# Layer-1 norms on one activation table, context statistics moved between the latent steps, and a gate weight piece moved ahead of the key rotation

## The chip, the cores and the metric

The kernel runs on one core of a Trainium2 chip. The metric is the device time of one execution in microseconds (us); lower is better. The engines are TensorE (PE, matmuls), VectorE (DVE), ScalarE (ACT), GpSimd (POOL) and SyncE (SP, which issues the DMAs). Each engine runs its own instructions in order, and they wait for one another by semaphores.

## What is computed

Two layers over 256 latent tokens and 256 context tokens with 1024 features. Layer 0 mixes with windowed attention and a gated recurrence, layer 1 with retention; each ends with a SwiGLU network. Ahead of every matrix product stands an RMS norm with a shift and a scale:

```python
def rms_norm(x, g=None):
    y = xf * lax.rsqrt(jnp.mean(xf * xf, axis=-1, keepdims=True) + EPS)
...
h_lat = modulate(rms_norm(x, norm_g[layer, 0]), m_lat[0], m_lat[1])
h_ctx = modulate(rms_norm(ctx, norm_g[layer, 0]), m_ctx[0], m_ctx[1])
...
q_l = apply_rope(to_heads(p['q'], RET_HEADS), cos, sin)
k_l = apply_rope(to_heads(p['k'], RET_HEADS), cos, sin) * k_scale
...
y_lat = gated_head_norm(o_fw + flip(o_bw), p['g']).astype(dt) @ w_out
```

## The kernel before

Features lie on the partitions and tokens along the free axis. Weights come in a fixed order as pieces of eight 128x128 blocks: SP loads a piece (`raw`, three buffers), ACT copies it to a rounded upper half (`whi`, L270) and DVE subtracts that from the raw piece for the lower half (`wlo`, L271), four buffers of each. A product is three matmuls: upper by upper (L343), upper weight by lower activation (L344), lower weight by upper activation (L345); where both halves of the activation lie side by side, two (L340 and L341).

Most code is written in program order and a list scheduler places instructions on the engines. On DVE and ACT the code of the first retention head (`ret_kq`, `ret_gate`, `ret_scores` for head 0) keeps its written order, which includes the norms that it drains first.

At the start of layer 1 there are two norms. The latent one (stream 0, lane `b`) keeps its matmuls ahead of its statistics: `pre` gives x times the gain, `first_group` multiplies four columns of weights by that (96 matmuls of 258 columns on `mm` banks, for two key and two query columns), and `fix` (L473, L474) applies the reciprocal root to the result. The same norm also builds the normed latents `hh`/`hl`, which the rest of the layer reads: for each of eight 128-feature slices `scaled` (L493, DVE), `shifted` (L499 on ACT for the upper half, L500 on DVE for the lower). The context norm (stream 1, lane `c`) has no `pre`; its eight steps of L493, L499, L500 must be done before the 48 context matmuls, which use the same weights and go to `ax` banks. `Norm.stats` is the statistics: a matmul with ones (L487), the logarithm (`ln`, L296 in the manual part) and the exponential (L490). `ln` loads the activation table for the logarithm (L294), and the table for the exponential is loaded ahead of L490.

After that come on DVE the four `fix` pairs, on ACT the bias of each (L1122), the rotation of the keys (`rope`, six DVE operations L1095 to L1097), two weight pieces by two calls of `ensure`, the rotation of the queries, and the splits; on TensorE the gate columns of head 0 (`ret_gate`) with the transposes of the normed tokens (`tok_lane`, L1110 and L1111) among them, and then the scores.

The norm ahead of the layer-1 FFN is the same class with `l = 1, j = 1`: `first_group` without context, latents only. There DVE's `join` additions (L357) and the FFN's products follow. `look` is how many pieces `ensure` prepares ahead.

Of the kernel before, what the change touches and what calls it, by code (L numbers as in the profile page):

```python
# [17 lines left out]
D = 1024  # L18
# [50 lines left out]
def hybrid_kernel(ctx, tc, xT, wst, mw0, mwT, small, cbc, cst, imask, dmat, out, order):  # L69
# [15 lines left out]
    def nm(s):  # L85
        uid[0] += 1
        return f"{s}_{uid[0]}"
# [7 lines left out]
    def mmb():  # L95
        return pm.tile([P, NT], F32, tag="mm", name=nm("mm"))
# [46 lines left out]
    epst = cp.tile([P, 1], F32, tag="eps", name="eps")  # L143
# [108 lines left out]
    pieces = {}  # L252
# [10 lines left out]
    def ensure(p):  # L263
        for q in range(len(pieces), min(p + look[0], N_PIECE - 1) + 1):
            r = q
            load_raw(r)
            src = raws.pop(r)
            hi = wp.tile([P, PIECE, P], F32R, tag="whi", name=nm("whi"))
            lo = wp.tile([P, PIECE, P], F32R, tag="wlo", name=nm("wlo"))
            A.activation(hi[:], src[:], AF.Copy)  # L270
            V.tensor_tensor(lo[:], src[:], hi[:].bitcast(F32), ALU.subtract)  # L271
            pieces[q] = (hi, lo)
# [26 lines left out]
    lanes = {}  # L299
# [23 lines left out]
    def drain(lane):  # L323
        q = lanes.get(lane, [])
        while q:
            for _ in q.pop(0):
                pass
# [19 lines left out]
    def cut(a, s):  # L347
        return (a[0][:, s], a[1][:, s])
# [53 lines left out]
    def first_group(src, cols, nl, hs, n_ctx):  # L402

        if nl.l > nl.j:
            look[0] = 0
            ensure(len(pieces))
            drain('b')
            ensure(len(pieces))
            drain('c')
        ps = [mmb() for _ in cols]  # L410
        ws = {}
        tail = 3 if nl.l and nl.j else 0
        todo = [(i, j) for i in range(KD - tail) for j in range(len(cols))]
        todo += [(i, j) for j in range(len(cols)) for i in range(KD - tail, KD)]
        for i, j in todo:
            ws[i, j] = take(src, i, cols[j])
            mm3(ps[j][:, 0:LW], ws[i, j], nl.p[i], i == 0, i == KD - 1)
        drain('b')
        lat = [nl.fix(p) for p in ps]
        drain('c')  # L420
        ctx = [(axb if j < FA else mmb)()[:, 0:L] for j in range(n_ctx)]
        if nl.l:
            todo = [(i, j) for i in K8 for j in range(n_ctx)]
        else:
            todo = [(i, j) for j in range(n_ctx) for i in K8]
        for i, j in todo:
            mm3(ctx[j], ws[i, j], cut(hs[i], CTX), i == 0, i == KD - 1)
        return lat, ctx
# [24 lines left out]
    class Norm:  # L453
# [31 lines left out]
        def stats(self):  # L485
            ps = axb()[:, 0:L]
            T.matmul(ps, ones, self.acc, start=True, stop=True)  # L487
            self.r = u()[:, 0:L]
            ln(self.r, ps, after=self.last, bias=epst[:], scale=1.0 / D)
            A.activation(self.r, self.r, AF.Exp, scale=-0.5)  # L490

        def scaled(self, k, t):
# [8 lines left out]

        def finish(self):
            self.stats()
            ahead = []
            for k in range(KD):
                if self.p:
                    yield
                t = u()[:, 0:L]
                self.scaled(k, t)
                ahead.append((k, t))  # L510
                if len(ahead) > (self.l > self.j):
                    self.shifted(*ahead.pop(0))
            for a in ahead:
                self.shifted(*a)
# [432 lines left out]
    for hd in range(4):  # L947
        c = E_H + 3 * hd
# [168 lines left out]
    def ret_kq(hd):  # L1117
        c = 12 * hd
        if hd == 0:
            lat, kc = first_group('oin', [c + O_K, c + O_K + 1, c + O_Q, c + O_Q + 1], n1[0], HS, 2)  # L1120
            for t, b in lat:
                A.activation(t, t, AF.Identity, bias=b)  # L1122
            (k0, _), (k1, _), (q0, _), (q1, _) = lat
            push('t', tok_lane())
        else:
            pk = group('oin', [c + O_K, c + O_K + 1], K8, HS, kouter=False)
            k0, k1 = pk[0][:, LAT], pk[1][:, LAT]
            kc = [pk[0][:, CTX], pk[1][:, CTX]]
        kf = [u(), u()]
        kk = []  # L1130
        rope([kf[0][:, LAT], kf[1][:, LAT]], k0, k1)
        qf = u((P, 2, L))
        if hd == 0:
            ensure(len(pieces))
            ensure(len(pieces))
            look[0] = LOOK
            rope([qf[:, 0, :], qf[:, 1, :]], q0, q1)
        for i in range(2):
            A.activation(kf[i][:, CTX], kc[i], AF.Copy)
            hi, lo = u(dt=F32R), u(dt=F32R)  # L1140
            split(kf[i][:], hi[:], lo[:])
            kk.append((hi[:], lo[:]))
        if hd:
            pq = group('oin', [c + O_Q, c + O_Q + 1], K8, HS, sls=(LAT,), kouter=False)
            q0, q1 = pq[0][:, LAT], pq[1][:, LAT]
            rope([qf[:, 0, :], qf[:, 1, :]], q0, q1)
        qhi, qlo = u((P, 2, L), F32R), u((P, 2, L), F32R)
        split(qf[:], qhi[:], qlo[:])
        return kk, (qhi, qlo)
# [240 lines left out]
```

## Time and profile before

| | |
|---|---|
| median of 3 runs | 1142.93 us (1140.12 to 1144.97) |
| profiled execution, whole | 1142.81 us |
| profiled execution, span of the trace | 1141.0 us, so 1.81 us lie around it |
| TensorE busy | 1112.6 us, 98% of the span |
| VectorE, ScalarE busy | 798.0 us (70%), 567.8 us (50%) |
| mean granted clock of TensorE | 0.994 |

The busy share of TensorE is not its peak, but the times at which it stands still are plain in the trace: what it waits for ends the kernel later. Times in the rows below are microseconds from the start of the span. PEclk is the clock that TensorE was granted, 1.00 for 2.4 GHz and 0.50 for 1.2 GHz.

### The profile page before, as it was taken

The numbers are of one execution on the slowest core, as the hardware profiler recorded it, in microseconds if no ns is written. First come the engines' busy times: TensorE is split into PE (matmuls) and PEld (weight loads), VectorE is DVE, ScalarE is ACT, GpSimd is POOL, SyncE is SP. The second block draws the span as 40 slices with busy tenths as digits, with TensorE's granted clock in tenths as the row PEclk, the third lists the DMA queues.
The fourth block names the chain that finished last, engine by engine and source line by source line (L and its number), as shares of the span: only waits on it lengthen the run. The fifth ranks groups of instructions, "written<-read, shape, count | busy, mean of one in ns | idle before, by whom it ended". The sixth has DMA issues, their size and how long they took to land.

```text
span 1141.0 us, 17472 instructions
## 1 busy us (share of the span) xinstructions
PE 1112.6 (98%) x6762; PEld 959.2 (84%) x6762; DVE 798.0 (70%) x1479; ACT 567.8 (50%) x996; POOL 20.9 (2%) x46
## 2 busy tenths in 40 slices
PE   3999999999999999999999998999999999999998
PEld 1777878888998888888888898999989889888887
DVE  3877698999798557347884568474747498767665
ACT  5676676673753222122232466454545566654651
POOL 0012000000000000000000000000000000000000
PEclk9899999999999999999999998999999999999999
DMA  9987212325327456247994323343434364665663
GB/s 327 353 236 185 93 57 75 101 86 186 109 95 250 138 161 207 75 129 221 316 311 128 95 91 111 111 130 121 125 125 131 110 185 156 212 186 185 187 186 108
DMA packets 56115, 182.37 MB, mean 160 GB/s; under 512 B 6368, under 2 KB 9824, under 8 KB 55904
## 3 DMA queue, kind: packets, MB, share of 16 engines
q1 hardware_dynamic: 53648, 176.45, 48.5%
q0 software_dynamic: 2240, 4.72, 1.7%
q8 instruction: 53, 0.87, 0.3%
q14 instruction: 30, 0.25, 0.1%
q10 hardware_dynamic: 144, 0.08, 0.0%
HBM read 177.56 MB, written 1.05 MB: 157 GB/s over the span
## 4 chain that ended last, share of the span: by engine, by line
PE 86%; DVE 8%; ACT 3%; issue 1%; DMA 1%; DVEq 0%; ACTq 0%; SPq 0%
PE mm L345 16%; PE mm L343 16%; PE mm L344 16%; PE mm L340 13%; PE mm L341 7%; PE ax L344 2%; PE ax L345 2%; PE ax L343 2%; PE ax L340 1%; DVE wlo L271 1%; PE ax L175 1%; DVE u L493 1%; PE ax L695 1%; DMA raw<-in_wst_dram 1%; PE ax L714 1%
## 5 line engine op out<-in xcount | busy, mean ns | idle before, releaser
L270 ACT ACTIVATE whi<-raw 128x1024 fp32r<-128x1024 f32 x230 | 243.1, 1058 | 358.5 <-PE mm L344 173.7
L271 DVE TENSOR_TENSOR wlo<-raw,whi 128x1024 fp32r<-128x1024 f32 x230 | 280.7, 1223 | 132.9 <-ACT whi L270 130.3
L343 PE MATMUL mm<-hh,whi 128*128 128x512 f32 (+1 forms) x752 | 273.3, 364 | 3.6 <-ACT whi L270 3.6
L344 PE MATMUL mm<-hl,whi 128*128 128x512 f32 (+1 forms) x752 | 272.7, 363 | 0.0
L345 PE MATMUL mm<-hh,wlo 128*128 128x512 f32 (+1 forms) x752 | 272.0, 362 | 0.5 <-DVE wlo L271 0.3
L343 PEld LDWEIGHTS mm<-hh,whi 128*128 128x128 f32 x752 | 144.0, 192 | 24.5 <-ACT whi L270 4.1
L345 PEld LDWEIGHTS mm<-hh,wlo 128*128 128x128 f32 x752 | 143.8, 191 | 22.0 <-DVE wlo L271 1.1
L344 PEld LDWEIGHTS mm<-hl,whi 128*128 128x128 f32 x752 | 144.0, 192 | 20.0 <-issue 0.2
L340 PE MATMUL mm<-u,whi 128*128 128x512 f32 x368 | 131.5, 398 | 0.5 <-DVE u L451 0.5
L344 PE MATMUL mm<-u,whi 128*128 128x512 f32 (+2 forms) x336 | 114.5, 341 | 0.0
L345 PE MATMUL mm<-u,wlo 128*128 128x512 f32 (+2 forms) x336 | 114.4, 341 | 0.0
L343 PE MATMUL mm<-u,whi 128*128 128x512 f32 (+2 forms) x336 | 114.1, 341 | 0.0
L340 PE MATMUL mm<-hh,whi 128*128 128x512 f32 x320 | 112.5, 396 | 0.9 <-DVE u L357 0.9
L341 PE MATMUL mm<-u,wlo 128*128 128x256 f32 x368 | 103.0, 280 | 0.0
L233 DVE CUSTOM_DVE_ANT_0 mr<-mr,cb 128x1024 f32<-128x1024 f32 x72 | 87.2, 1223 | 15.1 <-DMA mr<-in_mwT_dram 14.4
L341 PE MATMUL mm<-hh,wlo 128*128 128x256 f32 x320 | 89.4, 281 | 0.0
L340 PEld LDWEIGHTS mm<-u,whi 128*128 128x128 f32 x368 | 69.1, 188 | 16.3 <-DVE u L451 0.8
L340 PEld LDWEIGHTS mm<-hh,whi 128*128 128x128 f32 x320 | 60.0, 188 | 15.4 <-DVE u L357 1.2
L343 PEld LDWEIGHTS mm<-u,whi 128*128 128x128 f32 x336 | 63.5, 189 | 7.3
L341 PEld LDWEIGHTS mm<-u,wlo 128*128 128x128 f32 x368 | 69.5, 189 | 0.1
L344 PEld LDWEIGHTS mm<-u,whi 128*128 128x128 f32 x336 | 63.6, 189 | 7.0
L345 PEld LDWEIGHTS mm<-u,wlo 128*128 128x128 f32 x336 | 63.5, 189 | 7.1
(238 smaller groups left out, 1664.0 us busy)
## 6 DMA issues: line engine op xcount, KB each, us to landing
raw<-in_wst_dram SPq DMA_DIRECT2D x230, 512.0 KB, 3.7
mr<-in_mwT_dram SPq DMA_DIRECT2D x80, 512.0 KB, 4.6
u<-in_mw_dram SPq DMA_DIRECT2D x16, 256.0 KB, 5.2
u<-u POOLq DMA_DIRECT2D x20, 128.0 KB, 6.0
u<-in_dmat_dram POOLq DMA_DIRECT2D x8, 256.0 KB, 3.1
raw<-in_mw_dram SPq DMA_DIRECT2D x6, 256.0 KB, 5.2
mr<-in_mw_dram SPq DMA_DIRECT2D x6, 256.0 KB, 5.2
x<-in_xT_dram SPq DMA_DIRECT2D x8, 128.0 KB, 3.6
```

What stands on the lines that cost most here:

```text
L175: T.matmul(ps[32 * g:32 * g + 32, :], cT[:, k, :], mws[nt * 8 + k], start=(k < 4), stop=(k >= 4), skip_group_check=True)
L233: V.tensor_tensor_reduce(o, mr[:], cb[:, s, :], 1.0, 0.0, ALU.mult, ALU.add, mvec(l, s, ch, k))
L270: A.activation(hi[:], src[:], AF.Copy)
L271: V.tensor_tensor(lo[:], src[:], hi[:].bitcast(F32), ALU.subtract)
L340: T.matmul(o, w[0], a[2], start=first, stop=False, skip_group_check=True)
L341: anchor[0] = T.matmul(o[:, 0:L], w[1], a[0], start=False, stop=last, skip_group_check=True)
L343: T.matmul(o, w[0], a[0], start=first, stop=False, skip_group_check=shared)
L344: T.matmul(o, w[0], a[1], start=False, stop=False, skip_group_check=shared)
L345: anchor[0] = T.matmul(o, w[1], a[0], start=False, stop=last, skip_group_check=shared)
L493: V.scalar_tensor_tensor(t, xs(k, self.s), gsv[:, self.l, self.j, self.s, k:k + 1], self.r, ALU.mult, ALU.mult)
L695: T.transpose(tp[:, i, :], p[:, i * P:(i + 1) * P], ident)
L714: T.matmul(o[64 * j:64 * j + 64, col:col + P], vtok[:, kk, 64 * j:64 * j + 64], pts[3 * j + w][:, blk, :], start=(n == 0), stop=last, skip ...
```

## The change

The statistics of every layer-1 norm take one table that holds both functions. The context norm yields after its statistics, and `first_group` of the layer-1 mixer advances lane `b` three times and then lane `c` once before it drains `b`. One of the two `ensure` calls of `ret_kq` moves to the place right after `first_group`.

```diff
--- before.py
+++ after.py
@@ -404,6 +404,9 @@
         if nl.l > nl.j:
             look[0] = 0
             ensure(len(pieces))
+            for _ in range(3):
+                next(lanes['b'][0])
+            next(lanes['c'][0])
             drain('b')
             ensure(len(pieces))
             drain('c')
@@ -486,7 +489,7 @@
             ps = axb()[:, 0:L]
             T.matmul(ps, ones, self.acc, start=True, stop=True)
             self.r = u()[:, 0:L]
-            ln(self.r, ps, after=self.last, bias=epst[:], scale=1.0 / D)
+            ln(self.r, ps, after=self.last, exp=self.l > 0, bias=epst[:], scale=1.0 / D)
             A.activation(self.r, self.r, AF.Exp, scale=-0.5)
 
         def scaled(self, k, t):
@@ -501,6 +504,8 @@
 
         def finish(self):
             self.stats()
+            if self.l > self.j and not self.p:
+                yield
             ahead = []
             for k in range(KD):
                 if self.p:
@@ -1118,6 +1123,7 @@
         c = 12 * hd
         if hd == 0:
             lat, kc = first_group('oin', [c + O_K, c + O_K + 1, c + O_Q, c + O_Q + 1], n1[0], HS, 2)
+            ensure(len(pieces))
             for t, b in lat:
                 A.activation(t, t, AF.Identity, bias=b)
             (k0, _), (k1, _), (q0, _), (q1, _) = lat
@@ -1131,7 +1137,6 @@
         rope([kf[0][:, LAT], kf[1][:, LAT]], k0, k1)
         qf = u((P, 2, L))
         if hd == 0:
-            ensure(len(pieces))
             ensure(len(pieces))
             look[0] = LOOK
             rope([qf[:, 0, :], qf[:, 1, :]], q0, q1)
```

ScalarE at the start of layer 1, from the fifth latent step on (`hh_725` is the upper half of the fifth normed slice; `whi_1188` is the fourth weight piece of the group; `ax_1190` the context's sum of squares; `hh_717<-u_1192` the first context step). Before:

```order
L499 ACTIVATE hh_725_3430<-u_1183_6245,modv_175 128x256
L499 ACTIVATE hh_727_3432<-u_1184_6249,modv_175 128x256
L499 ACTIVATE hh_729_3434<-u_1185_6253,modv_175 128x256
L499 ACTIVATE hh_731_3436<-u_1186_6257,modv_175 128x256
L270 ACTIVATE whi_1188_6265<-raw_1187_6263 128x1024
L294 ACT_TABLE_LOAD
L296 ACTIVATE u_1191_6271<-ax_1190_6269,eps_173 128x256
L490 ACT_TABLE_LOAD
L490 ACTIVATE u_1191_6271<-u_1191_6271 128x256
L499 ACTIVATE hh_717_3422<-u_1192_6275,modv_175 128x256
L499 ACTIVATE hh_719_3424<-u_1193_6277,modv_175 128x256
```

And now (the fourth piece is `whi_1190` here, the context's sum `ax_1185`):

```order
L502 ACTIVATE hh_725_3430<-u_1183_6245,modv_175 128x256
L294 ACT_TABLE_LOAD
L296 ACTIVATE u_1186_6255<-ax_1185_6253,eps_173 128x256
L493 ACTIVATE u_1186_6255<-u_1186_6255 128x256
L502 ACTIVATE hh_727_3432<-u_1184_6249,modv_175 128x256
L502 ACTIVATE hh_729_3434<-u_1187_6259,modv_175 128x256
L502 ACTIVATE hh_731_3436<-u_1188_6263,modv_175 128x256
L270 ACTIVATE whi_1190_6271<-raw_1189_6269 128x1024
L502 ACTIVATE hh_717_3422<-u_1192_6275,modv_175 128x256
```

The context's table load, logarithm and exponential moved ahead of the sixth latent step, the load ahead of the exponential is gone, and the fourth weight piece comes after them.

VectorE behind the context steps, from the last `fix` (L474, `u_1210`) on; L1095 to L1097 (L1100 to L1102 in the changed file) are rotations. Before, both gate pieces (`wlo_1221`, `wlo_1224`) stand behind the keys' rotation:

```order
L474 TENSOR_TENSOR u_1210_6419<-mm_1203_6310,u_1173_6149 128x256
L1095 TENSOR_TENSOR u_1216_6479<-u_1204_6407,con_84 128x256
L1096 TENSOR_TENSOR u_1216_6479<-u_1206_6411,con_84 128x256
L1097 TENSOR_TENSOR u_1214_6477<-u_1216_6479 128x256
L1095 TENSOR_TENSOR u_1217_6483<-u_1206_6411,con_84 128x256
L1096 TENSOR_TENSOR u_1217_6483<-u_1204_6407,con_84 128x256
L1097 TENSOR_TENSOR u_1215_6478<-u_1217_6483 128x256
L271 TENSOR_TENSOR wlo_1221_6491<-raw_1219_6488,whi_1220_6490 128x1024
L271 TENSOR_TENSOR wlo_1224_6497<-raw_1222_6494,whi_1223_6496 128x1024
L1095 TENSOR_TENSOR u_1225_6500<-u_1208_6415,con_84 128x256
L1096 TENSOR_TENSOR u_1225_6500<-u_1210_6419,con_84 128x256
```

And now:

```order
L477 TENSOR_TENSOR u_1210_6419<-mm_1203_6310,u_1173_6149 128x256
L271 TENSOR_TENSOR wlo_1216_6476<-raw_1214_6473,whi_1215_6475 128x1024
L1100 TENSOR_TENSOR u_1219_6485<-u_1204_6407,con_84 128x256
L1101 TENSOR_TENSOR u_1219_6485<-u_1206_6411,con_84 128x256
L1102 TENSOR_TENSOR u_1217_6483<-u_1219_6485 128x256
L1100 TENSOR_TENSOR u_1220_6489<-u_1206_6411,con_84 128x256
L1101 TENSOR_TENSOR u_1220_6489<-u_1204_6407,con_84 128x256
L1102 TENSOR_TENSOR u_1218_6484<-u_1220_6489 128x256
L271 TENSOR_TENSOR wlo_1224_6497<-raw_1222_6494,whi_1223_6496 128x1024
L1100 TENSOR_TENSOR u_1225_6500<-u_1208_6415,con_84 128x256
```

The first gate piece (`wlo_1216`) moved ahead of the six operations of the keys' rotation; the second kept its place. TensorE at the same place, the first gate matmuls (`mm_1233` the first gate column, `mm_1234` the second). Before:

```order
L343 MATMUL mm_1233_6522<-hh_717_3422,whi_1220_6490 128x256
L344 MATMUL mm_1233_6522<-hl_718_3423,whi_1220_6490 128x256
L343 MATMUL mm_1234_6523<-hh_717_3422,whi_1223_6496 128x256
L344 MATMUL mm_1234_6523<-hl_718_3423,whi_1223_6496 128x256
L345 MATMUL mm_1233_6522<-hh_717_3422,wlo_1221_6491 128x256
L1110 MATMUL ax_1238_6533<-idr_6231,hh_717_3422 128x128
```

And now:

```order
L343 MATMUL mm_1233_6522<-hh_717_3422,whi_1215_6475 128x256
L344 MATMUL mm_1233_6522<-hl_718_3423,whi_1215_6475 128x256
L345 MATMUL mm_1233_6522<-hh_717_3422,wlo_1216_6476 128x256
L1115 MATMUL ax_1238_6533<-idr_6231,hh_717_3422 128x128
L1116 MATMUL ax_1238_6533<-idr_6231,hl_718_3423 128x128
```

The two matmuls of the second gate column that stood between now come later with the rest of that column.

VectorE in the layer-1 FFN's first group, from the `fix` of the last columns on (`wlo_1781` and `wlo_1784` are the third and fourth pieces of the next group of columns). Before:

```order
L473 COPY s_1767_9518<-mm_1740_9358 128x1
L474 TENSOR_TENSOR u_1766_9517<-mm_1740_9358,u_1745_9367 128x256
L493 SCALAR_TENSOR_TENSOR u_1768_9521<-x5_91,gsv_176,u_1745_9367 128x256
L493 SCALAR_TENSOR_TENSOR u_1769_9525<-x6_92,gsv_176,u_1745_9367 128x256
L493 SCALAR_TENSOR_TENSOR u_1770_9529<-x7_93,gsv_176,u_1745_9367 128x256
L500 SCALAR_TENSOR_TENSOR hh_1654_8905<-u_1768_9521,modv_175,hh_1654_8905 128x256
L500 SCALAR_TENSOR_TENSOR hh_1655_8906<-u_1769_9525,modv_175,hh_1655_8906 128x256
L500 SCALAR_TENSOR_TENSOR hh_1656_8907<-u_1770_9529,modv_175,hh_1656_8907 128x256
L271 TENSOR_TENSOR wlo_1781_9552<-raw_1779_9549,whi_1780_9551 128x1024
L271 TENSOR_TENSOR wlo_1784_9574<-raw_1782_9571,whi_1783_9573 128x1024
```

And now:

```order
L476 COPY s_1765_9514<-mm_1739_9357 128x1
L477 TENSOR_TENSOR u_1764_9513<-mm_1739_9357,u_1745_9367 128x256
L271 TENSOR_TENSOR wlo_1781_9552<-raw_1779_9549,whi_1780_9551 128x1024
L476 COPY s_1767_9518<-mm_1740_9358 128x1
L477 TENSOR_TENSOR u_1766_9517<-mm_1740_9358,u_1745_9367 128x256
L496 SCALAR_TENSOR_TENSOR u_1768_9521<-x5_91,gsv_176,u_1745_9367 128x256
L496 SCALAR_TENSOR_TENSOR u_1769_9525<-x6_92,gsv_176,u_1745_9367 128x256
L496 SCALAR_TENSOR_TENSOR u_1770_9529<-x7_93,gsv_176,u_1745_9367 128x256
L503 SCALAR_TENSOR_TENSOR hh_1654_8905<-u_1768_9521,modv_175,hh_1654_8905 128x256
L503 SCALAR_TENSOR_TENSOR hh_1655_8906<-u_1769_9525,modv_175,hh_1655_8906 128x256
L503 SCALAR_TENSOR_TENSOR hh_1656_8907<-u_1770_9529,modv_175,hh_1656_8907 128x256
L271 TENSOR_TENSOR wlo_1784_9574<-raw_1782_9571,whi_1783_9573 128x1024
```

The third piece moved from behind the last three slices' steps (three L493, three L500) to a place ahead of them.

## Rows read from the trace of the kernel before

**Rows 1.** Waits of TensorE by releaser: us in total, times, longest us.

```profile
PE ax L487 <- DVE u L483: 17.7, 2, 11.2
PE mm L343 <- ACT whi L270: 3.6, 3, 2.3
PE mm L340 <- DVE u L357: 0.9, 1, 0.9
```

**Rows 2.** Windows: us, busy of PE, PEld, DVE, ACT, POOL, PEclk, DMA share, GB/s.

```profile
691.00:691.50 0.50, 0.44 (x2) 0.24 (x2) 0.47 (x2) 0.50 (x1) 0.00 (x0) 0.93 0.00 0
691.50:698.00 6.50, 5.96 (x26) 5.67 (x27) 6.43 (x13) 3.92 (x8) 0.00 (x0) 0.50 0.51 161
698.00:698.50 0.50, 0.50 (x5) 0.50 (x5) 0.50 (x1) 0.27 (x1) 0.00 (x0) 0.75 0.00 0
909.00:911.00 2.00, 1.54 (x8) 1.36 (x9) 2.00 (x8) 1.98 (x5) 0.00 (x0) 1.00 0.69 219
972.00:974.00 2.00, 1.14 (x7) 0.77 (x6) 2.00 (x5) 1.84 (x4) 0.00 (x0) 1.00 0.39 70
```

**Rows 3.** Timeline of TensorE, context matmuls to scores: start us, us, instruction [idle before].

```profile
682.25 0.40 PE L343 MATMUL ax<-hh,whi 128*128 128x256 f32 x2
...
688.35 0.28 PE L345 MATMUL ax<-hh,wlo 128*128 128x256 f32 x1
690.94 0.39 PE L343 MATMUL mm<-hh,whi 128*128 128x256 f32 x1 [2.31 <-ACT whi L270]
...
692.83 0.58 PE L345 MATMUL mm<-hh,wlo 128*128 128x256 f32 x1
...
699.91 0.28 PE L343 MATMUL mm<-hh,whi 128*128 128x256 f32 x1
...
701.35 0.22 PE L1110 MATMUL ax<-idr,hh 128*128 128x128 f32 x1
...
702.20 0.33 PE L343 MATMUL mm<-hh,whi 128*128 128x256 f32 x1
...
703.33 0.28 PE L343 MATMUL ax<-u,u 128*128 128x256 f32 x1
```

**Rows 4.** Timeline of ScalarE, layer-1 norms.

```profile
666.07 1.28 ACT L490 ACT_TABLE_LOAD   x1
...
673.44 0.51 ACT L499 ACTIVATE hh<-u,modv 128x256 fp32r<-128x256 f32 x1 [0.62 <-DVE u L493]
...
676.23 1.04 ACT L270 ACTIVATE whi<-raw 128x1024 fp32r<-128x1024 f32 x1
...
678.59 0.47 ACT L296 ACTIVATE u<-ax,eps 128x256 f32<-128x256 f32 x1
...
680.38 0.42 ACT L490 ACTIVATE u<-u 128x256 f32<-128x256 f32 x1
```

**Rows 5.** Timeline of VectorE, context steps to key rotation.

```profile
680.83 0.88 DVE L493 SCALAR_TENSOR_TENSOR u<-u,gsv,u 128x256 f32<-128x256 f32 x2 [2.29 <-ACT u L490]
...
687.72 0.15 DVE L473 COPY s<-mm 128x1 f32<-128x1 f32 x1
...
689.30 0.41 DVE L1095 TENSOR_TENSOR u<-u,con 128x256 f32<-128x256 f32 x1
...
691.56 2.35 DVE L271 TENSOR_TENSOR wlo<-raw,whi 128x1024 fp32r<-128x1024 f32 x2
...
696.09 1.89 DVE L451 TENSOR_TENSOR u<-u,u 128x512 fp32r<-128x512 f32 x3
```

**Rows 6.** Timelines of VectorE, ScalarE, TensorE, start of layer-1 FFN.

```profile
964.54 2.36 DVE L271 TENSOR_TENSOR wlo<-raw,whi 128x1024 fp32r<-128x1024 f32 x2
...
970.36 1.06 ACT L270 ACTIVATE whi<-raw 128x1024 fp32r<-128x1024 f32 x1 [2.22 <-DMA raw<-in_wst_dram]
...
972.93 0.75 DVE L357 TENSOR_TENSOR u<-u,mm 128x256 f32<-128x256 f32 x2
...
973.40 0.50 PE L340 MATMUL mm<-hh,whi 128*128 128x512 f32 x1 [0.86 <-DVE u L357]
```

## The prediction

> **What bounds the kernel now.** I read the waits of TensorE first, because it is busy 98% of the span and whatever it stands still for is time at the end. Its longest waits, 17.7 us for L487, lie at the start of layer 0, which the change does not touch. Next comes L343 waiting for ACT's `whi` (3.6 us, longest 2.3 us), and a single wait of 0.9 us on DVE's L357 [rows 1]. The timeline of TensorE puts the 2.3 us at 690.94, between the context matmuls and the gate columns of layer 1 [rows 3], and the 0.86 us at 973.40, in the first groups of the layer-1 FFN [rows 6]. Then I read the granted clock in windows: it falls from 1.00 to 0.50 (from 2.4 to 1.2 GHz) at about 691.4 (0.93 in the half microsecond from 691.0) and returns at about 698.25, and both other short waits that I looked up, at 909 and at 972, leave it at 1.00 [rows 2]. Last I read ACT and DVE around 665 to 697, to see which chain ends the wait at 690.94.
>
> That chain is: context logarithm 678.59, table load, exponential 680.38, DVE's first context L493 at 680.83 (it had waited 2.29 us for that exponential) [rows 4, 5]; then eight context steps until the `fix` at 687.72, the keys' rotation from 689.30, and only at 691.56 the gate pieces' L271, the first of which lets L345 start at 692.83 [rows 3, 5]. TensorE had issued its last context matmul at 688.35.
>
> **The change at the start of layer 1.** What counts is how much earlier DVE can subtract the first gate piece.
>
> *Context statistics.* The fifth latent step stood at 673.44 [rows 4]. Its place is now about 0.3 us earlier: the first exponential comes 1.28 us earlier without its load, but DVE is then still subtracting the second weight piece, and ACT's copy of the third piece now follows the first latent step. I take 673.1; the bounds are 673.44 (no gain) and 672.5 (0.95, were DVE free). From there, with durations of rows 4 (ACT instructions overlap by some 0.1): step 0.51, load 1.28 to 674.94, logarithm 0.47 to 675.41, exponential 0.42 to 675.85, sixth latent step to 676.26; two DVE operations 0.40 apart (two L493 take 0.88 [rows 5]) to 677.17, eighth step to 677.70, fourth weight piece 1.06 (copies take 1.04 to 1.06 [rows 4, 6]) to 678.67, and its L271 about 1.23 (two take 2.35 [rows 5]) to 679.93. DVE overlaps by 0.08, so the first context L493 starts at 679.85 instead of 680.83: 0.98 us earlier. The load that is gone is 1.28 us [rows 4]; 0.3 us of it is lost because the fourth piece, done at 677.3 before, now lies in front of the context steps on both engines.
>
> The Trainium skill, "ScalarE: Activation LUTs", section What ACT_TABLE_LOAD costs, prices a switch of the set at 1283 ns for the load and about 1380 ns for a drain, 2.66 us together. The rows agree with the first part alone: 679.06, where the logarithm ends, to 680.38 is 1.32 us [rows 4]. By the page the load taken away would give some 1.3 us more, an estimate that would put the time near 1135.2 us.
>
> *The eight context steps* keep their pace (680.83 to 687.72 is 6.89 us [rows 5]), so the `fix` starts at 686.74 and ends as before 1.58 us later (687.72 to 689.30), at 688.32.
>
> *The gate piece.* ACT copies it at about 686.2 to 687.3, right behind the last context step, and DVE subtracts it at 688.32 to 689.55, ahead of the six rotation operations that took 689.30 to 691.56 before [rows 5]. L345 starts at 689.57 instead of 692.83. The piece's own load and its halves' buffers hold nothing up: the order of the SP and POOL queues is unchanged, and the buffer belongs to the first piece of the group, whose last reader is the second context step's matmuls.
>
> *TensorE.* Nothing that it reads before 679 changes place to its harm, so it reaches the context matmuls at 682.25 as before. They took 6.22 us because each follows a context step (two DVE operations, 0.79 us); 48 at 0.12 us (twelve take 1.44 us from 699.91 to 701.35 [rows 3]) are 5.76 us, and the steps are now 1 us ahead, so they end at 688.0. Two gate matmuls follow, then an idle gap of 1.3 us until 689.57; before, four matmuls stood in the 4.36 us from 688.47 to 692.83, which is 3.9 us idle.
>
> From L345 to the scores at 703.33 TensorE issued 68 matmuls, 44 of 256 columns and 24 of 128 (eight take 0.85 us, 701.35 to 702.20 [rows 3]). At the full clock that is 44 x 0.12 + 24 x 0.106 = 7.8 us; it took 10.5 us, so the half clock of rows 2 cost 2.7 us. If the clock stays at 1.00 over the shorter gap, 46 and 24 matmuls take 8.1 us and the scores start at 697.65, 5.7 us earlier.
>
> *What is late next.* DVE gains only 1.0 us here: keys' rotation 2.26 us to 691.8, second gate piece to 692.95, queries' rotation to 695.1, three splits of 1.89 us together to 697.0 (before 696.09 + 1.89 = 697.98 [rows 5]), 0.65 us before the scores need them. Behind them come the third gate piece (1.15 us to the next start) and two token splits (0.60 to the next, the last some 0.7), until about 699.35. TensorE wants the accumulator that the second of these frees twelve matmuls behind 697.65, at 699.1: I charge 0.2 us. So this place gives **5.5 us**; bounds are 4.5 (1 us of new waits of this sort) and 5.7.
>
> *The keys' rotation* starts 1.23 us later behind the gate piece's L271, but the chain ahead is 0.98 us shorter; what reads it (the splits, then the scores) has the 0.65 us above to spare. Without that cover it costs 0.3 us. The first latent exponential's load costs or gives nothing by itself: TensorE multiplies unnormed latents at that time.
>
> **The layer-1 FFN.** TensorE waits 0.86 us at 973.40 for DVE's L357 at 972.93. That stood behind the L271 of a piece whose copy waited 2.22 us for a DMA until 970.36 [rows 6]. This raw buffer is freed by the L271 of three pieces earlier, the first at 964.54 [rows 6]. It now stands ahead of three L493 and three L500, at least 6 x 0.40 = 2.4 us earlier, and the DMA with it. That covers the 0.86 us; nothing else waits there. The exponential without its load (1.28 us) helps the same steps. In exchange the second piece of the first such group comes about 1 us later, behind three latent steps; it is read only after the first piece's sixteen matmuls, so I charge nothing for it. I take **0.86 us**; bounds 0 and 1.0.
>
> **Sum.** 5.5 + 0.86 = 6.35 us. Against the profiled execution's 1142.81 us (span 1141.0 and 1.81 around it, 0.12 below the median of the runs shown) that is **1136.5 us**. A difference of 0.5%, 5.7 us, is about what a measurement of this kernel can tell from no change; the boundary is 1137.2 us.
>
> **The rivals.**
>
> *The clock falls over the shorter gap too.* For it: one gap in this stretch did bring it to 0.50. Against: that gap held 3.9 us idle in 4.4, while waits of 0.46 us (2.00 less 1.54) at 909 and 0.86 us at 972 kept 1.00 [rows 2]; 1.3 us is nearer to those. Price: 6.8 us at half rate (691.4 to 698.25) give back up to 3.4 us, 2.7 as before: 1136.5 + 3.1 = 1139.6 us. Chance 0.20.
>
> *The fourth weight piece comes late.* It moved behind a load, two functions and three latent steps; I have its upper half at 678.67 for a need at 682.25 - 24 x 0.12 = 679.37, and its lower half at 679.93 for 680.1 (TensorE's order now puts those lower matmuls three pairs later). Only 0.2 us are spare, and each microsecond beyond stops TensorE there and delays the context steps alike. A slip of 2 us gives 1138.3 us. Chance 0.10.
>
> *The FFN's wait stays* because L357 is held by something else: 1137.4 us. Chance 0.05.
>
> *Slower.* The same fourth piece, on ACT behind the context logarithm, slips far enough that the gap at 680 itself brings the clock down: a slip of s costs s and 3.4 us of half rate, which exceeds the 6.35 us from s = 3.0 us on; at 5 us the time is 1136.5 + 5 + 3.4 = 1144.9 us. For it speaks that the logarithm waits for a matmul and a DVE sum; against it that ACT has no other wait of that length in the walk. Chance 0.03.
>
> The order shows that the three loads and the moves are really there, so no change at all is not among them.
>
> **How the numbers follow.** The forecast has 0.62, 1136.5 us, and by the bounds of its terms 1136.1 (5.7 + 1.0) to 1138.3 (4.5 + 0). The range to 1140.2 takes in the clock's rival, the late piece to 3.7 us and the FFN's; below, 1134.2 leaves 1.9 us under the bounds for the spread of the runs before (2.8 us from the median down, 2.0 up). Faster by over 0.5% is about 0.7 of the forecast and little of the rest: 0.45. Slower by over 0.5% needs a slip beyond 8 us: 0.03. Within 0.5%: 0.52.
>
> **What would show it.** Right: no table load ahead of the exponential in the three layer-1 norms; L344 and L345 of the first gate column parted by a gap of about 1.3 us near 689; PEclk 1.00 from 685 to 705; the scores near 697.7; no wait on L357 near 967; a span of about 1134.7 us. Wrong: PEclk 0.50 behind 690, a TensorE wait on `whi` or `wlo` near 679 to 680, or waits of the transposes for their accumulators beyond 0.2 us.

## The result

The changed kernel takes 1134.47 us (median of 5, 1133.82 to 1135.71), beside 1141.72 us for the kernel before in the same rounds: a ratio of 0.9936, 95% interval 0.9917 to 0.9955. A second set on another occasion gave 1136.97 us and 0.9951 (0.9938 to 0.9965). The forecast of 1136.5 us lies between the two medians, and both lie inside its range of 1134.2 to 1140.2, the first by 0.3 us. Both intervals contain 0.995, so whether the gain is over 0.5% stays open. The profiled execution took 1135.25 us, its span 1133.5 us: 7.5 us less than the 1141.0 of before, where the sum had 6.35.

The waits of TensorE in the profile after, to hold against [rows 1]:

```profile
PE ax L490 <- DVE u L486: 17.7, 2, 11.2
PE mm L345 <- DVE wlo L271: 1.8, 2, 1.2
PE mm L343 <- ACT whi L270: 0.9, 1, 0.9
```

The 2.3 us wait for `whi` and the one for L357 are gone; what is left at the place of the change is 1.2 us for `wlo`. Windows of the same stage (columns as in [rows 2]):

```profile
685.00:688.00 3.00, 3.00 (x28) 3.00 (x27) 2.82 (x12) 2.71 (x5) 0.00 (x0) 1.00 0.00 0
688.00:690.00 2.00, 0.82 (x8) 0.62 (x7) 2.00 (x5) 2.00 (x5) 0.00 (x0) 1.00 0.00 0
690.00:698.00 8.00, 8.00 (x70) 8.00 (x70) 7.86 (x16) 4.48 (x9) 0.00 (x0) 1.00 0.44 131
698.00:705.00 7.00, 7.00 (x61) 7.00 (x61) 6.65 (x10) 6.06 (x9) 0.00 (x0) 1.00 0.66 200
```

PEclk stays at 1.00 through a gap in which TensorE is busy for 0.82 of 2.00 us. The timelines of ScalarE, VectorE and TensorE answer to [rows 4], [rows 5] and [rows 3]; first ScalarE after:

```profile
673.08 0.51 ACT L502 ACTIVATE hh<-u,modv 128x256 fp32r<-128x256 f32 x1 [0.62 <-DVE u L496]
673.61 1.28 ACT L294 ACT_TABLE_LOAD   x1
674.90 0.47 ACT L296 ACTIVATE u<-ax,eps 128x256 f32<-128x256 f32 x1
675.41 0.42 ACT L493 ACTIVATE u<-u 128x256 f32<-128x256 f32 x1
...
677.59 1.04 ACT L270 ACTIVATE whi<-raw 128x1024 fp32r<-128x1024 f32 x1
```

VectorE after:

```profile
678.67 1.23 DVE L271 TENSOR_TENSOR wlo<-raw,whi 128x1024 fp32r<-128x1024 f32 x1 [0.47 <-ACT whi L270]
679.81 0.88 DVE L496 SCALAR_TENSOR_TENSOR u<-u,gsv,u 128x256 f32<-128x256 f32 x2
...
686.69 0.15 DVE L476 COPY s<-mm 128x1 f32<-128x1 f32 x1
...
688.28 1.22 DVE L271 TENSOR_TENSOR wlo<-raw,whi 128x1024 fp32r<-128x1024 f32 x1
689.41 0.42 DVE L1100 TENSOR_TENSOR u<-u,con 128x256 f32<-128x256 f32 x1
```

TensorE after:

```profile
687.85 0.28 PE L345 MATMUL ax<-hh,wlo 128*128 128x256 f32 x1
...
689.55 0.39 PE L345 MATMUL mm<-hh,wlo 128*128 128x256 f32 x1 [1.18 <-DVE wlo L271]
...
697.84 0.28 PE L343 MATMUL ax<-u,u 128*128 128x256 f32 x1
```

The walk holds within 0.2 us at each step: fifth latent step 673.08 (forecast 673.1), lower half of the fourth piece 678.67 (678.67), first context step 679.81 (679.85), first fix 686.69 (686.74), gate piece 688.28 (688.32), L345 689.55 (689.57), scores 697.84 (697.65).

In the layer-1 FFN, to hold against [rows 6], VectorE and then ScalarE:

```profile
955.39 1.21 DVE L271 TENSOR_TENSOR wlo<-raw,whi 128x1024 fp32r<-128x1024 f32 x1
```

```profile
962.13 1.05 ACT L270 ACTIVATE whi<-raw 128x1024 fp32r<-128x1024 f32 x1
```

Part of the distance to [rows 6] is that this stage now starts 5.5 us earlier: its first pair of matmuls stands at 955.54, before at 961.03. Measured from that pair, the third piece of the group is subtracted 0.15 us ahead of it (before, 3.5 us behind it), and the copy that had waited 2.22 us for its DMA starts 6.6 us behind it (before, 9.3) and waits for none. The next two copies do wait for a DMA, 0.76 and 0.75 us, but TensorE does not feel it: it waits for no L357.

### The profile page after: what moved, and what is told of

It is laid out like the page before. It is cut to its first block, busy times and chain, and to the rows that moved or that the text cites. A ratio compares the mean times of both kernels' runs of the same rounds, so it can differ in the third digit from the quotient of the medians.

```text
span 1133.5 us, 17466 instructions
## 1 busy us (share of the span) xinstructions
PE 1107.2 (98%) x6762; PEld 954.5 (84%) x6762; DVE 798.1 (70%) x1479; ACT 563.5 (50%) x993; POOL 20.8 (2%) x46
## 4 chain that ended last, share of the span: by engine, by line
PE 91%; DVE 6%; ACT 1%; DMA 1%; issue 1%; DVEq 0%; ACTq 0%; SPq 0%
PE mm L345 17%; PE mm L344 17%; PE mm L343 17%; PE mm L340 14%; PE mm L341 7%; PE ax L344 3%; PE ax L345 3%; PE ax L343 3%; PE ax L340 1%; PE ax L175 1%; DVE wlo L271 1%; PE ax L700 1%; PE ax L719 1%; PE ax L341 1%; PE mm L448 1%; PE mm L446 1%
## 5 line engine op out<-in xcount | busy, mean ns | idle before, releaser
L271 DVE TENSOR_TENSOR wlo<-raw,whi 128x1024 fp32r<-128x1024 f32 x230 | 281.1, 1223 | 129.8 <-ACT whi L270 127.1
L345 PE MATMUL mm<-hh,wlo 128*128 128x512 f32 (+1 forms) x752 | 271.3, 361 | 1.8 <-DVE wlo L271 1.8
L345 PEld LDWEIGHTS mm<-hh,wlo 128*128 128x128 f32 x752 | 142.9, 190 | 22.8 <-DVE wlo L271 2.2
L340 PE MATMUL mm<-u,whi 128*128 128x512 f32 x368 | 131.3, 399 | 0.5 <-DVE u L454 0.5
L345 PE MATMUL mm<-u,wlo 128*128 128x512 f32 (+2 forms) x336 | 114.2, 341 | 0.0
L340 PE MATMUL mm<-hh,whi 128*128 128x512 f32 x320 | 111.9, 396 | 0.0
L340 PEld LDWEIGHTS mm<-u,whi 128*128 128x128 f32 x368 | 69.2, 188 | 16.3 <-DVE u L454 0.8
L340 PEld LDWEIGHTS mm<-hh,whi 128*128 128x128 f32 x320 | 60.1, 188 | 14.3
L345 PEld LDWEIGHTS mm<-u,wlo 128*128 128x128 f32 x336 | 63.5, 190 | 7.0
```

The lines of the kernel that those rows point to most:

```text
L340: T.matmul(o, w[0], a[2], start=first, stop=False, skip_group_check=True)
L345: anchor[0] = T.matmul(o, w[1], a[0], start=False, stop=last, skip_group_check=shared)
```

## The experiments

Below, a stand is a stretch in which an engine is idle, and the first gate L345 is the matmul that needs the lower half of the first gate piece. gate_only, table_only and ctx_only are the kernel before with one part of the change; no_gate and no_ctx are the changed kernel without one part; before_again, after_again and gate_again are second profiles of a kernel; the others are explained where they come.

So that kernels compare, the places are given in us from the start of the first table load (L294) of the layer-1 norms, which itself lies between 662.4 and 664.1. "Network" is the stretch from the first pair of matmuls of the layer-1 FFN to the last matmul. The column beside it takes out two paces of TensorE there, which the last experiments explain; it is good to about 0.1 us, since the pairs around a pause can be counted to either pace. The ratio is that to the kernel before in the same rounds.

| kernel | first context step | first gate L345 | scores | network | at one pace | ratio (95%) |
|---|---|---|---|---|---|---|
| before | 17.50 | 29.50 | 40.00 | 175.67 | 176.47 | |
| before_again | 17.49 | 29.49 | 40.12 | 177.02 | 177.29 | |
| changed | 16.54 | 26.28 | 34.57 | 173.61 | 175.34 | 0.9936 (0.9917 to 0.9955) |
| after_again | 16.53 | 26.27 | 34.56 | 175.21 | 175.34 | 0.9951 (0.9938 to 0.9965) |
| gate_only | 17.49 | 27.24 | 37.02 | 174.82 | 176.75 | 0.9975 (0.9966 to 0.9984) |
| gate_again | 17.50 | 27.24 | 37.04 | 175.19 | 177.12 | |
| table_only | 15.91 | 27.92 | 37.50 | 173.56 | 175.32 | 0.9971 (0.9959 to 0.9982) |
| ctx_only | 18.10 | 30.10 | 39.69 | 175.74 | 176.56 | 0.9995 (0.9986 to 1.0004) |
| no_gate | 16.53 | 28.53 | 39.12 | 173.56 | 175.32 | 0.9979 (0.9970 to 0.9988) |
| no_gate_warm | 16.54 | 28.54 | 36.60 | 173.75 | 175.33 | 0.9965 (0.9951 to 0.9978) |
| no_ctx | 15.91 | 25.65 | 33.95 | 173.75 | 175.33 | 0.9937 (0.9923 to 0.9951) |
| gate_in_fix | 16.55 | 25.26 | 33.54 | 173.56 | 175.28 | 0.9936 (0.9922 to 0.9949) |
| best | 15.92 | 24.85 | 33.05 | 174.67 | 175.32 | 0.9940 (0.9928 to 0.9953) |
| ffn_own_table | 16.53 | 26.27 | 34.57 | 175.54 | 176.32 | 0.9943 (0.9930 to 0.9955) |

### The gate piece alone (gate_only, gate_again)

```diff
             lat, kc = first_group('oin', ...)
+            ensure(len(pieces))
...
-            ensure(len(pieces))
             ensure(len(pieces))
             look[0] = LOOK
```

> The kernel before with one part of the change: one gate weight piece copied and subtracted right behind the first group, ahead of the keys' rotation. Tables and context statistics are as before. Theory (the stand of TensorE ahead of the first L345 sets the clock): DVE subtracts the piece from 689.30 (the end of the fixes before), so L345 starts near 690.55, and TensorE, which leaves the context matmuls at 688.47 and issues two gate matmuls, is idle for 1.84 us in place of 3.9. If the granted clock stays at 1.00 over that, the scores start near 690.55 + 8.29 = 698.8 (8.29 us is what the changed kernel took from that L345 to the scores), 4.5 us ahead of the kernel before; I put 0.6 on it. Rival one: 1.84 us is already long enough for the clock to fall as before, and only 2.3 us come. Rival two: it is the context chain that matters, and this part alone gives under 1 us. The 0.86 us wait of the layer-1 FFN on L357 stays in all of them.

L345 came 2.26 us earlier, as the theory had it, but the clock fell: rival one in kind, with less lost than before. The second profile repeats the place and the fall.

> The kernel with the early gate piece alone once more, for a second profile. Its stand of 1.69 us brought the clock down for 3.3 us in the first. Theory one: it falls again (then 1.69 us are too long in this place, and 1.18 us are not). Theory two: it stays at 1.00 this time (then a stand of that length is on the edge, and chance decides).

TensorE in gate_again, then its windows:

```profile
690.35 0.39 PE L345 MATMUL mm<-hh,wlo 128*128 128x256 f32 x1 [1.69 <-DVE wlo L271]
```

```profile
691.00:692.00 1.00, 1.00 (x9) 1.00 (x8) 1.00 (x3) 0.48 (x1) 0.00 (x0) 0.67 0.56 160
692.00:693.00 1.00, 1.00 (x6) 1.00 (x6) 0.97 (x3) 0.77 (x3) 0.00 (x0) 0.50 0.76 311
693.00:694.00 1.00, 1.00 (x7) 1.00 (x6) 1.00 (x3) 0.28 (x1) 0.00 (x0) 0.50 0.14 53
694.00:695.00 1.00, 1.00 (x7) 1.00 (x7) 0.97 (x4) 0.00 (x0) 0.00 (x0) 0.62 0.41 45
```

A stand of 1.69 us lost the clock in both profiles, one of 1.18 us kept it in all three with that stand (changed, after_again, ffn_own_table). The stretch at 0.50 is 3.4 us here (0.66 of the first row, two whole rows, 0.76 of the last), where it was 6.8 us before [rows 2]. From L345 to the scores it is 9.78 us (37.02 - 27.24) against 8.29 in the changed kernel: 1.5 us lost.

### The table alone, the statistics alone (table_only, ctx_only)

```diff
-            ln(self.r, ps, after=self.last, bias=epst[:], scale=1.0 / D)
+            ln(self.r, ps, after=self.last, exp=self.l > 0, bias=epst[:], scale=1.0 / D)
```

> The kernel before with one part of the change: logarithm and exponential of the layer-1 norms from one table. Theory: the first context L493 comes 1.28 us earlier (near 679.55), all behind it with it, L345 of the first gate column near 691.55; TensorE ends the context matmuls near 688.0 and is still idle for some 3 us, so the clock falls to 0.50 as before and layer 1 gives 1.3 us. The FFN's wait on L357 (0.86 us) goes, since the third piece's subtraction moves ahead of the last slices there: 2.1 us in all. Rival one: the clock stays, and about 4 us + 0.86 come, so that the table is the main part of the change. Rival two: the FFN's wait stays, 1.3 us in all.

The context chain gained 1.59 us, not 1.28, and the clock fell for 3.4 us; with the FFN's wait gone the time is about 3.3 us less (0.9971), where 2.1 was expected. ScalarE of table_only:

```profile
676.08 1.04 ACT L270 ACTIVATE whi<-raw 128x1024 fp32r<-128x1024 f32 x1
677.14 1.28 ACT L294 ACT_TABLE_LOAD   x1
678.43 0.47 ACT L296 ACTIVATE u<-ax,eps 128x256 f32<-128x256 f32 x1
678.94 0.42 ACT L490 ACTIVATE u<-u 128x256 f32<-128x256 f32 x1
```

The exponential follows the logarithm at once, and the first norm's missing load lets the latent steps run 0.3 us ahead (the copy in the first of these rows stands 12.60 us behind the first load, before 12.90 [rows 4]). 1.28 + 0.3 is all of the gain: the drain that the Trainium skill ("ScalarE: Activation LUTs", section What ACT_TABLE_LOAD costs) adds to a load shows in no row here.

```diff
+            for _ in range(3):
+                next(lanes['b'][0])
+            next(lanes['c'][0])
             drain('b')
...
             self.stats()
+            if self.l > self.j and not self.p:
+                yield
```

> The kernel before with one part of the change: the context statistics between the fifth and the sixth latent step, with their two table loads; gate pieces and tables as before. Theory (this part costs): the fourth weight piece and the last three latent steps now stand behind logarithm, exponential and two loads, so the fourth piece ends some 1.3 us later than in the changed kernel (its lower half near 681.3), TensorE waits about 1 us for it near 680, and the first context L493 comes at 18.1 us behind the first layer-1 table load, in place of 17.50: 0.6 us slower at L345, the clock falls as before, and the whole is 0.3 to 1.0 us slower than the kernel before. Rival: the move is a gain by itself, as I had it in the sum, and the first context L493 comes before 17.5.

The theory, to the row: the first context step stands at 18.10, and TensorE of ctx_only waits for the fourth piece:

```profile
679.61 0.39 PE L343 MATMUL mm<-u,whi 128*128 128x258 f32 x1 [0.81 <-ACT whi L270]
...
690.84 0.39 PE L343 MATMUL mm<-hh,whi 128*128 128x256 f32 x1 [2.02 <-ACT whi L270]
```

L345 is 0.60 us later than before. The scores are 0.31 us earlier all the same, because this time the clock was at 0.50 for 3.4 us and not for 6.8; the ratio is that of no change, and the 0.3 to 1.0 us that were expected at the end did not come.

### Without one part (no_gate, no_ctx)

no_gate puts the moved `ensure` back:

> The changed kernel without one part: both gate pieces stand again behind the keys' rotation. Theory: the context steps start at 679.8 as in the changed kernel, fixes end at 688.3, the rotation at 690.55, and L345 starts near 691.85; TensorE has been idle for some 3.4 us, the clock falls to 0.50 as before, and what stays against the kernel before is the 1.0 us of the context chain and the 0.86 us of the FFN: 1.9 us. Rival: the clock falls only beyond what this kernel's stand is, and 1.0 + 2.7 + 0.86 = 4.6 us stay.

L345 at 28.53 and scores at 39.12 are the theory: of the gain at this place 0.88 us is left, since the clock is at 0.50 for 6.8 us again.

no_ctx takes the `next` lines and the `yield` out of the changed kernel:

> The changed kernel without one part: the context statistics stand again behind the eighth latent step and the fourth weight piece; one table and the early gate piece stay. Measured from the start of the table load of the first layer-1 norm, the first context L493 came at 17.50 us in the kernel before, 16.54 with the whole change, 16.53 with everything but the gate piece, and 15.91 with the table alone. Theory: the table alone is what moves the context chain, and the move of the statistics takes 0.6 us of it back (the fourth piece now ends ahead of the context steps on VectorE). So this kernel has its first context L493 at 15.9, L345 0.6 us earlier than the changed kernel (at 25.7), the stand ahead of it at about 0.6 us in place of 1.18, the clock at 1.00, and scores up to 0.6 us earlier: 0 to 0.6 us less than the changed kernel. Rival: the move is needed, since TensorE now waits for the fourth piece or for context steps, and this kernel is some 1 us slower than the changed one.

L345 is 0.62 us earlier than with the whole change, the scores too, and no wait takes its place. So this part of the change costs 0.6 us; its ratio (0.9937) can't be told from the changed kernel's, as 0.6 us is below what the rounds resolve.

### Is it the idle time? (no_gate_warm)

```diff
         for i, j in todo:
             mm3(ctx[j], ws[i, j], cut(hs[i], CTX), i == 0, i == KD - 1)
+        if nl.l > nl.j:
+            for i in K8:
+                w, a = ws[i, 1], cut(hs[i], CTX)
+                T.matmul(ctx[1], w[0], a[0], start=i == 0, stop=False)
+                T.matmul(ctx[1], w[0], a[1], start=False, stop=False)
+                T.matmul(ctx[1], w[1], a[0], start=False, stop=i == KD - 1)
...
-            ensure(len(pieces))
...
+            ensure(len(pieces))
             ensure(len(pieces))
             look[0] = LOOK
```

> The changed kernel with both gate pieces behind the keys' rotation, and with 24 matmuls that nobody needs: the context product of the second key column is computed once more into the same accumulator, behind the first time, so that TensorE works 2.9 us longer in the place where it stands for the gate piece. The result is the same. Theory (an idle TensorE is what brings the clock down): the stand ahead of L345 shrinks from some 3.4 us to about 0.4, L345 itself stays where it was without these matmuls (28.5 us behind the first layer-1 table load), the clock stays at 1.00, and the scores come some 2.5 us earlier than without the 24 matmuls (36.6 in place of 39.1 us behind that load). Rival: the clock falls at this place for another reason (the work that follows, or the time since its last fall), and the scores stay at 39.1 or come later.

The order of all other instructions is that of no_gate, L345 stands where it stood (28.54 and 28.53), and the scores are at 36.60, 2.52 us earlier. Windows of 685 to 700, of no_gate, no_gate_warm, gate_only and the changed kernel:

```profile
685.00:700.00 15.00, 12.63 (x79) 11.93 (x78) 13.97 (x32) 9.77 (x17) 0.00 (x0) 0.77 0.30 82
```

```profile
685.00:700.00 15.00, 14.70 (x125) 14.50 (x124) 14.68 (x33) 11.19 (x19) 0.00 (x0) 1.00 0.30 83
```

```profile
685.00:700.00 15.00, 13.31 (x98) 13.02 (x97) 14.68 (x35) 10.63 (x19) 0.00 (x0) 0.89 0.20 70
```

```profile
685.00:700.00 15.00, 13.82 (x118) 13.62 (x117) 14.68 (x33) 11.19 (x19) 0.00 (x0) 1.00 0.29 83
```

Matmuls that nobody needs, put into the gap, keep PEclk at 1.00 and give back 2.5 us with VectorE's chain untouched. So the clock here followed TensorE's idle time, and the long half-rate stretch cost 2.5 us.

### A version that gains more at the place (gate_in_fix, best)

```diff
-        lat = [nl.fix(p) for p in ps]
+        lat = []
+        for p in ps:
+            lat.append(nl.fix(p))
+            if nl.l > nl.j and len(lat) == 1:
+                ensure(len(pieces))
...
             lat, kc = first_group('oin', ...)
-            ensure(len(pieces))
```

> The changed kernel with the first gate piece one step further ahead: its subtraction stands behind the first of the four fixes, not behind the fourth. Theory: it starts when its copy is done (687.2), L345 starts near 688.4 and the last stand of TensorE there (1.18 us) is gone; but DVE has as much to do ahead of the splits as before (they end at 697.0 in the changed kernel, against scores at 697.84) and ahead of the two token splits behind them (699.3), so the scores come at most 0.85 us earlier and the fourth transposes wait for their accumulator: 0.3 us less than the changed kernel, between 0 and 0.85. Rival one: all of the 1.18 us comes. Rival two: the fixes that now come 1.2 us later hold something else up, and it is slower than the changed kernel.

> The changed kernel with the statistics of the context back behind the eighth latent step, and the first gate piece behind the first of the four fixes. Theory: both gains add, so that the first context L493 is at 15.9 us behind the first layer-1 table load, L345 waits for nothing (TensorE's own end of the context matmuls is the bound), and all of VectorE's work ahead of the scores ends 0.6 us earlier than with the gate piece in the fixes alone: scores near 33.0 us behind that load, 1.6 us less than the changed kernel, of which the waits for splits and accumulators behind take up to 0.6: 1.0 to 1.6 us less in all. Rival: VectorE is the bound from there on, nothing comes, and it is within 0.3 us of the changed kernel.

best is gate_in_fix without the move of the statistics. Both did what they should up to the scores (33.54 and 33.05 against 34.57), and gave 0.6 to 0.9 us of it back by the network's start: most of it at the second score matmul and at the fourth transposes, where TensorE has caught up with VectorE's splits (in best one wait of 0.15 us is listed there, at 698.36). At the network's start gate_in_fix is 0.2 us ahead of the changed kernel by the trace, as expected, and best 0.9 us, a little under the 1.0 to 1.6 expected of it; no_ctx, which only leaves out the move of the statistics, has 0.6 of that. The ratios agree within their intervals, so no better version is shown by the time as a whole.

### The network of layer 1 (ffn_own_table, after_again, before_again)

```diff
-            ln(..., exp=self.l > 0, ...)
+            ln(..., exp=self.l > self.j, ...)
```

> The changed kernel, but the norm ahead of the layer-1 network loads a table of its own for the exponential again; both norms at the start of layer 1 keep the shared one. Theory: the load (1.28 us) puts the third weight piece of the first group back behind the last slices' steps, the DMA of its raw buffer starts later, and TensorE waits some 0.9 us on DVE's L357 again: 0.9 us more than the changed kernel in the network of layer 1 (from the first pair of matmuls to the end, corrected for the stretches at 0.3467 and 0.3533 us per pair), and nothing else changes. Rival: the wait is not there, since the early start of layer 1 or the order of the pieces removed it, and the time is that of the changed kernel.

The wait came back, 0.72 us, the network took 1.0 us more at one pace (176.32 - 175.34), and ScalarE's copy again waits for a late DMA. TensorE, then ScalarE:

```profile
967.18 0.50 PE L340 MATMUL mm<-hh,whi 128*128 128x512 f32 x1 [0.72 <-DVE u L357]
```

```profile
964.14 1.06 ACT L270 ACTIVATE whi<-raw 128x1024 fp32r<-128x1024 f32 x1 [2.08 <-DMA raw<-in_wst_dram]
```

That copy is the one which the changed kernel starts at 962.13 without a wait.

> The changed kernel once more, beside the others and with a second profile. The extra 1.1 us by which its first profile beat the forecast lay in the network of layer 1, where pairs of matmuls (512 and 256 columns) went every 0.3467 us in some stretches and every 0.3533 us in others. Theory one: which stretch has which is a matter of the kernel; then this profile has 0.3533 from 955 to 1009, 0.3467 to 1099 and 0.3533 from there, as the first had. Theory two: it is chance in each execution; then the stretches differ.

Starts of L340 twelve pairs apart in the changed kernel, first profile, then second:

```profile
1049.61 0.39 PE L340 MATMUL mm<-hh,whi 128*128 128x512 f32 x1
...
1053.77 0.39 PE L340 MATMUL mm<-hh,whi 128*128 128x512 f32 x1
```

```profile
1049.72 0.40 PE L340 MATMUL mm<-hh,whi 128*128 128x512 f32 x1
...
1053.96 0.40 PE L340 MATMUL mm<-hh,whi 128*128 128x512 f32 x1
```

4.16 against 4.24 us for the same twelve pairs of one kernel at PEclk 1.00: theory one fails. The pace changes only at a few places, mostly where TensorE paused for a tenth of a microsecond or more. The first profile had about 90 us of its network at 0.3467 us per pair, the second 2 to 7; the kernel before had 41 and then 9 to 14. Theory two, chance in each execution, is not shown by that: gate_only and gate_again are one kernel as well, and both had 0.3467 over the same 89 us (1014.9 to 1104.3 and 1013.7 to 1103.1). What decides stays open.

> The kernel before once more, for a second profile. Theory: the clock falls again behind the stand at the first gate piece, since the stand is the same 3.9 us; where exactly it falls and for how long (6.8 us in the first profile, 3.3 us in the kernels with a single part) may differ, and the stretches of the layer-1 network at 0.3467 and 0.3533 us per pair differ by chance. Rival: both are a matter of the kernel and come as in the first profile.

The fall of the clock came as before (6.8 us), the pace did not; the L357 wait was longer:

```profile
974.95 0.50 PE L340 MATMUL mm<-hh,whi 128*128 128x512 f32 x1 [1.64 <-DVE u L357]
```

Each us at the quick pace saves 0.0192 us (0.3533 / 0.3467 - 1). Put to one pace, by the table, the network takes 175.28 to 175.34 us in all eight profiles with the shared table there, and 176.32 to 177.29 us in all six without it.

## Why the forecast held, and where it was off

**The start of layer 1** was forecast at 5.5 us and gave 5.43 (40.00 - 34.57). Its parts add up at L345: 1.58 us from the table (29.50 - 27.92), 2.25 from the gate piece (28.53 - 26.28), less 0.62 for the move of the statistics (26.27 of after_again - 25.65), together 3.21 of the measured 3.22. The other 2.21 us are the clock: 10.50 us from L345 to the scores before, 8.29 after, though two matmuls more (0.24 us) now stand there. No single part gets all of it: the table or the gate piece alone leaves a stand that still brings the clock down, for 1.5 us.

**Context statistics.** The 0.98 us of the forecast was 0.96 in the result, yet as a net: the step set 1.28 us for the load against 0.3 lost to the fourth piece. The table alone gives 1.59 and the move takes 0.62 of it. The walk itself was right; the split was not. I had priced the loss that the move brings and not asked what the chain does without it: the move is no gain but a cost.

**The clock.** That 1.3 us keep 1.00 was right, with less room than the argument gave: 1.69 us did not. The prediction's 3.9 us of idle before are counted from start to start at 0.12 us a matmul; the trace lists waits of 2.31 [rows 3] and 0.44 us in that gap, and these are what compares with 1.18 and 1.69. The rival's price of 3.1 us was too high for that case; a stand of 1.69 us cost 1.5 us. The half clock of before, 2.7 us in the sum, is 2.5 us by no_gate_warm.

**Fourth piece.** No wait of TensorE stands near 680 in the changed kernel, so 0.2 us of slack sufficed, and less was left: the lower half ends at 679.90 (678.67 + 1.23), and its first matmul starts at 679.97. With the two loads of ctx_only it was overrun by 0.81 us.

**What is late next.** The 0.2 us charged for the transposes' accumulator did not come as a wait. From the scores to the first pair of the network it is 257.7 us in both kernels. The matmuls from L345 took 8.29 us where the sum had 8.08: two errors of the same size cancel, which is luck.

**The layer-1 FFN** is the term that was mis-sized: "I take 0.86 us; bounds 0 and 1.0". The mechanism was right, the size was not, for two reasons. First, the sum took the listed idle time as the whole price. In the kernel before, the L340 on either side of the one that waits start at

```profile
972.02 0.40 PE L340 MATMUL mm<-hh,whi 128*128 128x512 f32 x1
...
973.85 0.40 PE L340 MATMUL mm<-hh,whi 128*128 128x512 f32 x1
```

These two pairs take 1.83 us, where two pairs otherwise take 0.71: the wait costs 1.12 us, and its row [rows 6] lists 0.86. Second, the stand varies, 0.7 to 1.6 us in the six profiles without the shared table there, because TensorE races a DMA: the L271 that frees the raw buffer stands 3.5 us behind the network's first pair in all six, the copy that waits for the DMA starts 9.2 to 9.95 us behind it, and at the quick pace TensorE is at L357 sooner. The edit gives 1.0 to 2.0 us at one pace, 1.4 in the mean (176.75 - 175.32), and 1.13 between the two first profiles (176.47 - 175.34).

**The 1.2 us beyond the sum** between those two profiles: the last matmul starts at 1136.70 and 1129.15, 7.55 us apart. That is 0.06 ahead of layer 1, 5.43, 1.13, and 0.93 of pace (49 us more at 0.0192), in all 7.55. Without the pace 6.6 us are left, against 6.35. The pace was no term of the prediction, and that it came out in favour of the changed kernel is luck: the two profiles of that kernel differ by 1.6 us in the network (175.21 - 173.61). Its two medians are 2.5 us apart, more than the pace accounts for in the profiles; what the rest is stays open.

## What to carry to other kernels

Where an engine stands idle, price two things apart: the stand, and the clock behind it, which comes back only when what is left of the stand is short enough (1.18 us here; 1.69 was too long). So the worth of a part depends on what stands beside it: the gate piece gave 3.0 us to the scores alone (40.00 - 37.02) and 4.6 on top of the other two parts (39.12 - 34.57), since only then the clock stayed. Undo each part of a change by itself and read it at a landmark of its own stage: a part that costs 0.6 us can hide in a net gain, and a time at the end of 1.1 ms can't show it. A stage of dense matmuls can differ by 1.6 us between two executions of one kernel, so one pair of profiles doesn't settle a microsecond.

## What the runs showed of the hardware

- Pairs of matmuls of 512 and 256 columns go every 0.3467 or every 0.3533 us at a granted clock of 1.00, for tens of microseconds, and change between the two at small pauses; two executions of one kernel can differ in it (changed, before) or agree (gate_only). What selects the pace stays open.
- The stretch at 0.50 lasted 6.8 us behind the stands of before and no_gate, and 3.4 us behind those of gate_only, table_only and ctx_only. It did not follow the length of the stand: ctx_only waited 2.02, 0.44 and 0.44 us there and had 3.4 us, no_gate waited 1.78, 0.45 and 0.15 us and had 6.8. Why the one or the other was not tried.
- A stand of 1.69 us ahead of L345 brought the clock down twice; one of 1.64 us at L357 in before_again left it at 1.00, as the windows of before_again around it show, and so did the five shorter ones at that place in other profiles. Whether the length, the work around or chance decides between them stays open.

```profile
972.00:974.00 2.00, 1.31 (x8) 0.91 (x6) 1.00 (x1) 2.00 (x5) 0.00 (x0) 1.00 0.40 162
974.00:976.00 2.00, 1.05 (x6) 0.92 (x7) 2.00 (x5) 1.84 (x3) 0.00 (x0) 1.00 0.39 66
976.00:980.00 4.00, 4.00 (x25) 3.49 (x24) 3.74 (x7) 2.63 (x6) 0.00 (x0) 1.00 0.77 237
```
